# Moving a block's operand sums and its last norm to VectorE, reordering seven products, and keeping split weights in DRAM

## The chip, the cores and the metric

The kernel runs on one core of a Trainium2 chip. The metric is device time in microseconds (us) of one execution. The core has five engines that each run their own list of instructions in order: TensorE (PE, matmul; its weight loads are listed as PEld), VectorE (DVE), ScalarE (ACT), GpSimd (POOL) and SyncE (SP), which here only issues DMAs. ACT and POOL can issue DMAs too, from the same ordered list as their arithmetic.

## The reference, cut to what matters

The reference is one layer over 2048 tokens of width 1024. In short:

```python
h = layer_norm(x, emb_ln_g, emb_ln_b)
z = h @ w_in                                # 1024 x 1536: 512 columns for the S5 mixer, 1024 for the gated mixer
mix = concat(rms(s5(z[..., :512])), rms(sgu(z[..., 512:]))) @ w_out
h = layer_norm(ALPHA * h + mix, ln1_g, ln1_b)
ffn = (silu(h @ w_ffn_gate) * (h @ w_ffn_up)) @ w_ffn_down       # inner width 2816
ple = (p @ w_ple) * sigmoid(h @ w_ple_gate + b_ple_gate)
out = layer_norm(ALPHA * h + ffn + ple, ln2_g, ln2_b)
```

All of it is float32.

## The kernel before, in words

**Precision.** Each float32 product is made of three passes on TensorE (`mm3`, L69 to L71). For that every operand is split in two: a rounded high part by a cast on ScalarE (L64) and the remainder by a subtract on VectorE (L65). A tile of 128 x 512 therefore costs one cast and one subtract before PE can use it.

**Phase A (0 to about 430 us).** Four chunks of 512 tokens go through the input norm, the input projection and the gated mixer; the S5 mixer follows. `w_stream` yields 48 pieces of `w_in`, 128 x 1024 floats (512 KB) each: four for the S5 columns of chunk 0, then for each chunk eight for the gated mixer and four for the S5 columns of the next chunk; the last eight belong to chunk 3. So 12 distinct pieces come four times. Three are loaded in `norm_in`; the other 45 pass through `ahead_w`, which keeps up to three pieces ahead: a load into a `raw` buffer (3 of them, one load each), then two casts and two subtracts into two `wsp` tiles (6 of them). For five pieces (`POOL_W`) the subtract is on POOL. POOL also builds rotation tables in this phase (L683 to L703).

**Phase B (540 us to the end).** The tokens go in two blocks of 1024, block 0 and block 1, and each block is a 2 x 2 arrangement: the first and the second 512 tokens (`tg` 0 and 1), each with a left and a right half of the columns (`hf`). A large product is done with seven half-size products instead of eight (Strassen-Winograd), for which sums of operands are needed. For each block come: the gate of the `ple` branch (`ple`), eleven steps of gate and up projection with seven products each, and the down projection (`down`), where product n adds its result to one quarter of the accumulators `acc`.

**The operand sums.** `operands(blk)` loads h of the block from DRAM (`load_f`, tile `tx`, 6 buffers), splits it, and for four values of j calls `sums_B`, which forms four sums on POOL (L1358 to L1361) and splits them. For block 1 this runs while block 0 is in its down projection: `phase_b` advances it by one step after each of the seven products, but the framework that lays out the instruction lists puts work earlier where an engine has room, and in the trace all of it lies between about 1255 and 1340 us, in the first two products.

**The down projection.** `seven` runs the products in the order 0 to 6 on two sets of four PSUM banks: even ones accumulate in `u`, odd ones in `q` (1 starts one set, 3 and 5 share the next). After each product, `read` adds the four banks to `acc` on VectorE (L1500). A product is 11 steps of two operand loads on SP (L1467, L1468), two splits, and 12 matmuls. In block 1, product 6 takes its four banks one after the other, so that the token tiles of `tg` 1 finish one by one.

**The last norm.** `norm_out` has four steps `pr` of two token tiles: statistics and inverse root on VectorE; then, for all but the second half of block 1, the scaling on ScalarE (L1297) and gain and bias on POOL (L1303, L1304, 128 x 512 at a time); then the store of the tile on SP (L1306). For the second half of block 1 VectorE does it all in two instructions per 128 x 512 (`ln_apply`, L136 and L137). After product 5, `down` runs the first two steps (`tg` 0). In block 0 the other two run inside the `ple` of block 1, in block 1 after everything else. The `ple` of block 1 begins with `rows`, whose first instruction is a memset on POOL (L1263).

Of the kernel before, what the change touches and what calls it, by code (L numbers as in the profile page):

```python
# [7 lines left out]
F32 = mybir.dt.float32  # L8
F32R = mybir.dt.float32r
I32 = mybir.dt.int32  # L10
AF = mybir.ActivationFunctionType
ALU = mybir.AluOpType

P = 128
# [18 lines left out]
POOL_W = range(3, 16, 3)  # L33
# [17 lines left out]
class Kern:  # L51
# [100 lines left out]
    def run(self):  # L152
        nc, tc = self.nc, self.tc
        with ExitStack() as ctx:
# [15 lines left out]
            self.tbd = dt([NG * NS, 2, NC + 1], F32, name="tbd")  # L170
            self.hfd = dt([4, D, 512], F32, name="hfd")
            self.xnd = dt([S, D], F32, name="xnd")
            self.fod = dt([2, NP, 7, P, 512], F32, name="fod")
            self.wtd = dt([NP, 2, P, D], F32, name="wtd")
            self.pgd = dt([4, 2, P, D], F32, name="pgd")
# [170 lines left out]

    def ahead_w(self, n=W_AHEAD):
        while len(self.ahead) < n:
            w = next(self.ws, None)
            if w is not None:  # L350
                self.wi += 1
                w = self.load_split(w, 1024, self.nc.gpsimd if self.wi in POOL_W else None)
            self.ahead.append(w)

    def next_w(self):
# [776 lines left out]

    def seven(self, product, read):
        u = [self.bank() for _ in range(4)]
        product(0, u, True)
        read(0, u)
        yield
        for n in range(1, 7):  # L1140
            if n % 2:
                if n < 5:
                    q = [self.bank() for _ in range(4)]
                product(n, q, n < 5)
                read(n, q)
            else:
                product(n, u, False)
                read(n, u)
            yield

    def ple(self, blk, operands, accs):

# [51 lines left out]
                bias(ps, hf)  # L1204
                sig(tg, hf, ps, True)

        for n, _ in enumerate(self.seven(product, read)):
            yield
        for tg in range(2):
            c0 = blk * 1024 + tg * 512  # L1210
# [62 lines left out]
    def norm_out(self, blk, accs):  # L1273

        nc, v, a = self.nc, self.nc.vector, self.a
        last = blk == 1
        gb = []
        for nm in ("ln2_g", "ln2_b"):
            gb.append([self.t512() for _ in range(2)])
            for hf in range(2):  # L1280
                nc.sync.dma_start(out=gb[-1][hf],
                                  in_=a[nm][0][hf * 512:(hf + 1) * 512].unsqueeze(0).broadcast_to([P, 512]))
        for pr in range(4):
            tg, t0 = pr // 2, 2 * (pr % 2)
            xs = accs[tg][t0:t0 + 2]
            parts = [[x] for x in xs] if last and tg else [xs]
            for i, part in enumerate(parts):
                mv = self.ln_stats(part, D)
                rs = self.ln_rstd(mv)
                for j, x in enumerate(part):  # L1290
                    t = t0 + i + j
                    nb = None
                    if not (last and tg):
                        nb = self.small.tile([P, 1], F32, name="nb", tag="nb", bufs=3)
                        v.tensor_scalar(out=nb, in0=mv[:, j, 0:1], scalar1=rs[:, j:j + 1], scalar2=-1.0,
                                        op0=ALU.mult, op1=ALU.mult)
                        nc.scalar.activation(out=x, in_=x, func=AF.Identity, scale=rs[:, j:j + 1], bias=nb)  # L1297
                    for hf in range(2):
                        xh = x[:, hf * 512:(hf + 1) * 512]
                        if nb is None:  # L1300
                            self.ln_apply(xh, xh, mv[:, j, 0:1], rs[:, j:j + 1], gb[0][hf], gb[1][hf])
                        else:
                            nc.gpsimd.tensor_tensor(out=xh, in0=xh, in1=gb[0][hf], op=ALU.mult)  # L1303
                            nc.gpsimd.tensor_tensor(out=xh, in0=xh, in1=gb[1][hf], op=ALU.add)  # L1304
                    c0 = blk * 1024 + tg * 512 + t * P
                    nc.sync.dma_start(out=self.out[0][c0:c0 + P, :], in_=x)  # L1306
            yield
# [45 lines left out]
        return h  # L1353

    def sums_B(self, blk, B, j):
        g = self.nc.gpsimd
        b11, b12, b22, b21 = (self.load_f(blk, tg, k) for tg, k in ((0, j), (1, j), (1, j + 4), (0, j + 4)))
        g.tensor_tensor(out=b22, in0=b22, in1=b12, op=ALU.subtract)  # L1358
        g.tensor_tensor(out=b12, in0=b12, in1=b11, op=ALU.subtract)
        g.tensor_tensor(out=b11, in0=b22, in1=b11, op=ALU.add)  # L1360
        g.tensor_tensor(out=b21, in0=b21, in1=b11, op=ALU.subtract)  # L1361
        for i, t in ((3, b12), (4, b11), (5, b22), (6, b21)):
            B[i][j] = self.split_f(t, self.hTt() if 4 * j + i - 3 < 14 else self.hxt())
# [91 lines left out]
    def down(self, blk, accs, tail):  # L1455
# [40 lines left out]
        def read(n, ps):  # L1496
            tg, hf = ((0, 0), (0, 0), (0, 1), (1, 1), (1, 1), (0, 1), (1, 0))[n]
            for t in range(4):
                x = accs[tg][t][:, hf * 512:(hf + 1) * 512]
                v.tensor_tensor(out=x, in0=x, in1=ps[t], op=ALU.add)  # L1500

        for n, _ in enumerate(self.seven(product, read)):
            if n == 5:
                next(tail)
                next(tail)
            yield

# [29 lines left out]
```

## Time and profile before

| | us |
|---|---|
| median of three runs (lowest, highest) | 2291.97 (2288.82, 2292.2) |
| the profiled execution | 2291.72 |
| its span in the trace | 2289.9 |
| PE busy | 2160.6 |
| DVE busy | 1569.8 |
| ACT busy | 887.6 |
| POOL busy | 671.6 |
| mean granted TensorE clock | 0.978 |

The span is what the trace covers from the first to the last recorded work; the profiled execution lasted 1.8 us longer. A matmul of 512 columns is listed with some 0.39 us, but they overlap: in an undisturbed stretch of 20 us about 90 of them start, one each 0.22 us. So the number of matmuls in a stretch tells more about lost time than PE's busy time.

### The profile page before, as it was taken

What the parts mean: (1) busy time and instruction counts of PE and PEld (TensorE: products, weight loads), DVE (VectorE), ACT (ScalarE), POOL (GpSimd) and SP (SyncE); (2) the same over time, 40 slices, a digit from 0 to 9 for tenths busy, and PEclk for the clock granted to TensorE, in tenths of its full rate; (3) what the DMA queues carried; (4) which work ended last, traced back from release to release, by engine and by line L of the source; (5) the groups of instructions that cost most, each with busy time, mean ns of one, the idle gap of its engine ahead of it and who ended that gap; (6) DMA issues with size and microseconds to landing.
All of it is one profiled execution on the core that took longest, in us unless ns stands there. A gap on an engine that the chain in (4) does not pass through costs nothing.

```text
span 2289.9 us, 27942 instructions
## 1 busy us (share of the span) xinstructions
PE 2160.6 (94%) x9556; PEld 1762.1 (77%) x9556; DVE 1569.8 (69%) x2724; ACT 887.6 (39%) x1511; POOL 671.6 (29%) x602
## 2 busy tenths in 40 slices
PE   7899998899899899999999889989999999999996
PEld 6777887777677778888888668868788888878885
DVE  7997779777786455666666675663576767665559
ACT  4444554353324433232323444444333333324442
POOL 1187200000004024454545220052246455410004
PEclk9999999999999999999999999989999999999998
DMA  8546444547975434545454766543243434346563
GB/s 268 148 152 219 139 139 143 154 113 239 312 249 202 156 127 135 175 161 180 165 172 164 249 201 207 183 138 129 79 143 120 143 115 144 101 139 211 193 200 131
DMA packets 314124, 385.81 MB, mean 168 GB/s; under 512 B 62406, under 2 KB 180214, under 8 KB 313980
## 3 DMA queue, kind: packets, MB, share of 16 engines
q1 hardware_dynamic: 262812, 318.45, 43.3%
q10 hardware_dynamic: 50080, 61.36, 7.6%
q0 software_dynamic: 1088, 4.21, 0.5%
q8 instruction: 75, 1.23, 0.2%
q14 instruction: 69, 0.57, 0.1%
HBM read 273.30 MB, written 110.64 MB: 168 GB/s over the span
## 4 chain that ended last, share of the span: by engine, by line
PE 66%; DVE 14%; DMA 8%; issue 7%; POOL 3%; ACT 2%; SPq 0%; ACTq 0%; DVEq 0%; POOLq 0%
PE ps L69 21%; PE ps L70 21%; PE ps L71 21%; DMA tx<-hfd 1%; DVE st L116 1%; DVE wsp L65 1%; DMA raw<-md 1%; PE ps L143 1%; DVE z L912 1%; DMA U<-ud 1%; DVE hTx L65 1%; POOL acc L1303 1%; DVE hT L65 1%; DVE acc L1044 1%; POOL acc L1304 0%
## 5 line engine op out<-in xcount | busy, mean ns | idle before, releaser
L65 DVE TENSOR_TENSOR wsp<-raw,wsp 128x512 fp32r<-128x512 f32 x463 | 397.1, 865 | 296.3 <-ACT wsp L64 291.2
L64 ACT CAST wsp<-raw 128x512 fp32r<-128x512 f32 x473 | 290.6, 622 | 559.5 <-PE ps L71 348.3
L69 PE MATMUL ps<-hT,wsp 128*128 128x512 f32 x744 | 290.7, 391 | 6.0 <-ACT hT L312 6.0
L70 PE MATMUL ps<-hT,wsp 128*128 128x512 f32 x744 | 290.4, 391 | 1.0 <-DVE hT L313 1.0
L71 PE MATMUL ps<-hT,wsp 128*128 128x512 f32 x744 | 290.0, 390 | 0.0
L69 PE MATMUL ps<-wsp,ff 128*128 128x512 f32 x636 | 252.0, 396 | 20.7 <-ACT ff L64 20.7
L71 PE MATMUL ps<-wsp,ff 128*128 128x512 f32 x636 | 251.2, 396 | 6.7 <-DVE ff L65 6.6
L70 PE MATMUL ps<-wsp,ff 128*128 128x512 f32 x636 | 251.0, 395 | 0.2 <-DVE wsp L65 0.2
L69 PE MATMUL ps<-hTx,wsp 128*128 128x512 f32 x616 | 241.5, 392 | 5.7 <-DVE tx L1406 3.7
L70 PE MATMUL ps<-hTx,wsp 128*128 128x512 f32 x616 | 239.9, 389 | 0.0
L71 PE MATMUL ps<-hTx,wsp 128*128 128x512 f32 x616 | 239.7, 389 | 0.0
L64 ACT CAST wsp<-S 128x512 fp32r<-128x512 f32 x158 | 97.9, 620 | 240.6 <-PE ps L71 162.2
L1373 POOL TENSOR_TENSOR S<-raw 128x512 f32<-128x512 f32 x44 | 68.5, 1557 | 408.6 <-DVE wsp L65 258.6
L70 PE MATMUL ps<-wsp,hT 128*128 128x512 f32 x416 | 165.1, 397 | 6.0 <-DVE wsp L65 6.0
L69 PE MATMUL ps<-wsp,hT 128*128 128x512 f32 x416 | 165.8, 399 | 4.8 <-DVE z L912 4.8
L65 DVE TENSOR_TENSOR wsp<-S,wsp 128x512 fp32r<-128x512 f32 x158 | 129.7, 821 | 56.3 <-ACT wsp L64 54.3
L69 PEld LDWEIGHTS ps<-hT,wsp 128*128 128x128 f32 x744 | 140.2, 188 | 35.3 <-ACT hT L312 6.5
L71 PE MATMUL ps<-wsp,hT 128*128 128x512 f32 x416 | 164.5, 395 | 0.0
L70 PEld LDWEIGHTS ps<-hT,wsp 128*128 128x128 f32 x744 | 140.2, 188 | 31.0 <-DVE hT L313 2.2
L71 PEld LDWEIGHTS ps<-hT,wsp 128*128 128x128 f32 x744 | 140.1, 188 | 29.0
L69 PEld LDWEIGHTS ps<-wsp,ff 128*128 128x128 f32 x636 | 121.6, 191 | 48.9 <-ACT ff L64 24.2
L1303 POOL TENSOR_TENSOR acc<-acc,t 128x512 f32<-128x512 f32 x24 | 36.7, 1547 | 398.4 <-ACT acc L1297 398.4
(345 smaller groups left out, 4267.6 us busy)
## 6 DMA issues: line engine op xcount, KB each, us to landing
raw<-fod SPq DMA_DIRECT2D x126, 256.0 KB
raw<-in_w_in_dram SPq DMA_DIRECT2D x48, 512.0 KB
raw<-in_w_ffn_gate_dram SPq DMA_DIRECT2D x44, 512.0 KB
raw<-in_w_ffn_up_dram SPq DMA_DIRECT2D x44, 512.0 KB
fod<-tx ACTq DMA_DIRECT2D x88, 256.0 KB
raw<-wtd SPq DMA_DIRECT2D x72, 256.0 KB
fod<-ff ACTq DMA_DIRECT2D x66, 256.0 KB
tx<-hfd SPq DMA_DIRECT2D x56, 256.0 KB
```

What stands on the lines that cost most here:

```text
L64: nc.scalar.copy(out=hi, in_=src)
L65: (e or nc.vector).tensor_tensor(out=lo, in0=src, in1=hi.bitcast(F32), op=ALU.subtract)
L69: mm(ps, lhsT=lh, rhs=rh, start=start, stop=False, skip_group_check=more)
L70: mm(ps, lhsT=lh, rhs=rl, start=False, stop=False, skip_group_check=more)
L71: mm(ps, lhsT=ll, rhs=rh, start=False, stop=stop, skip_group_check=more)
L116: nc.vector.bn_stats(out=st[:, c, :], in_=t[:, c * 512:(c + 1) * 512])
L143: self.nc.tensor.transpose(ps[:, t * P:(t + 1) * P], x[:, col:col + P], self.ident)
L912: v.scalar_tensor_tensor(out=mx[:, ct, :].rearrange("p (c s) -> p s c", s=L), in0=yT[ct].rearrange("p (s c) -> p s c", s=L), scalar=self.g ...
L1044: v.tensor_tensor(out=x, in0=x, in1=ag0, op=ALU.mult)
L1303: nc.gpsimd.tensor_tensor(out=xh, in0=xh, in1=gb[0][hf], op=ALU.mult)
L1373: g.tensor_tensor(out=s1, in0=a21, in1=a22, op=ALU.add)
```

## The change

It has three parts.

1. `ahead_w`: the 12 pieces of `w_in` numbered 4 to 15 (chunk 0's gated mixer and chunk 1's S5 columns) are loaded and split as before, and the two split tiles of each are also stored to a new DRAM buffer `wsd`, by DMAs that ScalarE issues. From piece 16 on (32 pieces) nothing is split: SP loads the two finished `wsp` tiles (512 KB each) straight from `wsd`.
2. `seven` takes the order as an argument. `ple` keeps 0 to 6; `down` uses 0, 1, 2, 3, 5, 4, 6. The first two steps of the last norm come one after product 5 and one after product 4, instead of both after product 5.
3. `norm_out` always uses `ln_apply` on VectorE; `sums_B` of block 1 is on VectorE (that of block 0 stays on POOL).

```diff
             self.xnd = dt([S, D], F32, name="xnd")
+            self.wsd = dt([12, 2, P, 2, 512], F32, name="wsd")
...
         while len(self.ahead) < n:
-            w = next(self.ws, None)
-            if w is not None:
+            src = next(self.ws, None)
+            w = None
+            if src is not None:
                 self.wi += 1
-                w = self.load_split(w, 1024, self.nc.gpsimd if self.wi in POOL_W else None)
+                at = self.wsd[(self.wi - 4) % 12] if self.wi > 3 else None
+                if self.wi < 16:
+                    w = self.load_split(src, 1024, self.nc.gpsimd if self.wi in POOL_W else None)
+                    if at is not None:
+                        for i, t in enumerate(w.tiles):
+                            self.nc.scalar.dma_start(out=at[i], in_=t.bitcast(F32))
+                else:
+                    w = Wide([self.wspt() for _ in range(2)])
+                    for i, t in enumerate(w.tiles):
+                        self.nc.sync.dma_start(out=t.bitcast(F32), in_=at[i])
             self.ahead.append(w)
...
-    def seven(self, product, read):
...
+    def seven(self, product, read, order):
+        for n in order:
+            start = n in (0, 1, 3)
+            if start:
+                ps = [self.bank() for _ in range(4)]
+                if n == 0:
+                    u = ps
+                else:
+                    q = ps
+            ps = q if n % 2 else u
+            product(n, ps, start)
+            read(n, ps)
+            yield n
...
                 for j, x in enumerate(part):
                     t = t0 + i + j
-                    nb = None
-                    if not (last and tg):
-                        nb = self.small.tile([P, 1], F32, name="nb", tag="nb", bufs=3)
-                        v.tensor_scalar(out=nb, in0=mv[:, j, 0:1], scalar1=rs[:, j:j + 1], scalar2=-1.0,
-                                        op0=ALU.mult, op1=ALU.mult)
-                        nc.scalar.activation(out=x, in_=x, func=AF.Identity, scale=rs[:, j:j + 1], bias=nb)
                     for hf in range(2):
                         xh = x[:, hf * 512:(hf + 1) * 512]
-                        if nb is None:
-                            self.ln_apply(xh, xh, mv[:, j, 0:1], rs[:, j:j + 1], gb[0][hf], gb[1][hf])
-                        else:
-                            nc.gpsimd.tensor_tensor(out=xh, in0=xh, in1=gb[0][hf], op=ALU.mult)
-                            nc.gpsimd.tensor_tensor(out=xh, in0=xh, in1=gb[1][hf], op=ALU.add)
+                        self.ln_apply(xh, xh, mv[:, j, 0:1], rs[:, j:j + 1], gb[0][hf], gb[1][hf])
...
     def sums_B(self, blk, B, j):
-        g = self.nc.gpsimd
+        g = self.nc.vector if blk else self.nc.gpsimd
...
-        for n, _ in enumerate(self.seven(product, read)):
-            if n == 5:
-                next(tail)
+        for n in self.seven(product, read, (0, 1, 2, 3, 5, 4, 6)):
+            if n in (5, 4):
                 next(tail)
             yield
```

## Rows read from the trace of the kernel before

**Rows 1.** The page, part 1: busy time, share of the span, instructions.

```profile
PE 2160.6 (94%) x9556; PEld 1762.1 (77%) x9556; DVE 1569.8 (69%) x2724; ACT 887.6 (39%) x1511; POOL 671.6 (29%) x602
```

**Rows 2.** Stretches: length, PE, PEld, DVE, ACT, POOL busy (count), clock, DMA share, GB/s.

```profile
1260.00:1280.00 20.00, 16.69 (x74) 13.32 (x72) 16.23 (x27) 8.07 (x14) 0.00 (x0) 1.00 0.70 206
1280.00:1300.00 20.00, 18.53 (x69) 14.74 (x70) 12.07 (x18) 9.90 (x18) 6.03 (x4) 0.83 0.85 303
1300.00:1320.00 20.00, 17.20 (x74) 13.56 (x74) 10.72 (x15) 8.14 (x15) 5.89 (x4) 1.00 0.75 258
1320.00:1340.00 20.00, 13.43 (x47) 9.27 (x47) 19.58 (x19) 10.98 (x21) 13.11 (x8) 0.83 0.52 167
1500.00:1520.00 20.00, 10.68 (x34) 7.31 (x33) 5.25 (x6) 5.50 (x8) 13.04 (x10) 0.80 0.43 146
1520.00:1540.00 20.00, 20.00 (x78) 16.23 (x77) 18.65 (x62) 8.76 (x13) 3.04 (x3) 0.86 0.47 158
1540.00:1560.00 20.00, 20.00 (x88) 16.01 (x87) 10.37 (x13) 9.72 (x14) 19.74 (x14) 1.00 0.29 106
2050.00:2070.00 20.00, 16.22 (x64) 12.61 (x63) 13.11 (x20) 7.43 (x13) 0.00 (x0) 0.91 0.81 277
2070.00:2090.00 20.00, 20.00 (x90) 16.57 (x89) 11.34 (x18) 9.03 (x16) 0.00 (x0) 1.00 0.64 208
```

**Rows 3.** A wait, 1255 to 1345: who waited for whom, total us, times, longest.

```profile
ACT hT L64 <- POOL tx L1359: 9.6, 4, 3.3
```

**Rows 4.** Groups of instructions, whole span: busy us, mean ns, idle before.

```profile
L1358 POOL TENSOR_TENSOR tx<-tx 128x512 f32<-128x512 f32 x8 | 12.1, 1516 | 87.9 <-DMA tx<-hfd 78.9 <-DMA raw<-fod 9.0
L1449 DVE TENSOR_TENSOR tx<-tx 128x512 f32<-128x512 f32 x22 | 15.0, 684 | 0.0
```

**Rows 5.** Waits, 1480 to 1530, SP's own first.

```profile
SPq L1306 <- POOL acc L1304: 21.4, 4, 6.1
...
ACT wsp L64 <- DMA raw<-wtd: 9.1, 1, 9.1
```

**Rows 6.** Group of the last norm's gain on POOL (the bias is alike).

```profile
L1303 POOL TENSOR_TENSOR acc<-acc,t 128x512 f32<-128x512 f32 x24 | 36.7, 1547 | 398.4 <-ACT acc L1297 398.4
```

**Rows 7.** Timeline of the end: start us, us, engine, instruction.

```profile
2271.75 0.39 PE L71 MATMUL ps<-hTx 128*128 128x512 f32 x1
2277.69 0.68 DVE L1500 TENSOR_TENSOR acc<-acc,ps 128x512 f32<-128x512 f32 x1
2284.60 1.42 DVE L137 SCALAR_TENSOR_TENSOR acc<-acc,rs,t 128x512 f32<-128x512 f32 x2
```

**Rows 8.** Timeline of product 5's end; then one wait of the whole span.

```profile
2235.26 3.39 DVE L65 TENSOR_TENSOR hT<-raw,hT 128x512 fp32r<-128x512 f32 x5 [0.58 <-ACT hT L64]
2238.06 0.39 PE L69 MATMUL ps<-hT 128*128 128x512 f32 x1
2238.56 2.47 DVE L1500 TENSOR_TENSOR acc<-acc,ps 128x512 f32<-128x512 f32 x4
...
PE ps L69 <- DVE tx L1406: 3.7, 10, 0.4
```

**Rows 9.** Stretches of phase A, columns as in the first such group.

```profile
40.00:125.00 85.00, 76.41 (x359) 62.44 (x359) 83.16 (x223) 38.36 (x63) 22.40 (x41) 0.94 0.57 172
125.00:205.00 80.00, 73.70 (x346) 60.87 (x345) 64.06 (x119) 35.16 (x59) 66.35 (x123) 0.96 0.57 178
285.00:430.00 145.00, 133.86 (x673) 111.05 (x672) 126.48 (x273) 70.18 (x169) 2.23 (x6) 0.99 0.50 147
148.00:158.00 10.00, 10.00 (x59) 8.65 (x57) 5.80 (x13) 6.28 (x12) 9.22 (x35) 1.00 1.02 386
```

**Rows 10.** Phase A: a timeline row, a group (125 to 205 us), a DMA issue.

```profile
178.83 0.79 PE L70 MATMUL ps<-wsp,hT 128*128 128x512 f32 x1 [5.03 <-DVE wsp L65]
...
L65 DVE TENSOR_TENSOR wsp<-raw,wsp 128x512 fp32r<-128x512 f32 x23 | 17.1, 770 | 10.4 <-ACT wsp L64 10.4
...
1266.46 0.33 ACTq L1434 DMA_DIRECT2D fod<-tx  x1
```

More of the change, by code (lines that the diff above doesn't have):

```diff
@@ L1131, in down_sums @@
         self.nc.sync.dma_start(out=self.wtd[i, 1], in_=rB)
-    def seven(self, product, read):
[L1136 to L1145, printed above, removed]
-            else:
-                product(n, u, False)
-                read(n, u)
-            yield
+    def seven(self, product, read, order):
[11 more added lines that the diff above has]
+            yield n
     def ple(self, blk, operands, accs):
@@ L1205, in read @@
                 sig(tg, hf, ps, True)
-        for n, _ in enumerate(self.seven(product, read)):
+        for _ in self.seven(product, read, range(7)):
             yield
@@ L1291, in norm_out @@
                     t = t0 + i + j
-                    nb = None
-                    if not (last and tg):
-                        nb = self.small.tile([P, 1], F32, name="nb", tag="nb", bufs=3)
-                        v.tensor_scalar(out=nb, in0=mv[:, j, 0:1], scalar1=rs[:, j:j + 1], scalar2=-1.0,
-                                        op0=ALU.mult, op1=ALU.mult)
-                        nc.scalar.activation(out=x, in_=x, func=AF.Identity, scale=rs[:, j:j + 1], bias=nb)
                     for hf in range(2):
                         xh = x[:, hf * 512:(hf + 1) * 512]
-                        if nb is None:
-                            self.ln_apply(xh, xh, mv[:, j, 0:1], rs[:, j:j + 1], gb[0][hf], gb[1][hf])
-                        else:
-                            nc.gpsimd.tensor_tensor(out=xh, in0=xh, in1=gb[0][hf], op=ALU.mult)
-                            nc.gpsimd.tensor_tensor(out=xh, in0=xh, in1=gb[1][hf], op=ALU.add)
+                        self.ln_apply(xh, xh, mv[:, j, 0:1], rs[:, j:j + 1], gb[0][hf], gb[1][hf])
                     c0 = blk * 1024 + tg * 512 + t * P
@@ L1500, in read @@
                 v.tensor_tensor(out=x, in0=x, in1=ps[t], op=ALU.add)
-        for n, _ in enumerate(self.seven(product, read)):
-            if n == 5:
-                next(tail)
+        for n in self.seven(product, read, (0, 1, 2, 3, 5, 4, 6)):
+            if n in (5, 4):
                 next(tail)
```

## The prediction

> **What bounds the kernel now.** The first view is the page's busy times: PE is busy for 94% of the span, VectorE for 69% [rows 1]. So the time is PE's work plus the stretches in which PE is held up, and a change that takes no matmul away can only win from those. The table of 20 us stretches shows where they are. An undisturbed stretch of the down projection starts 90 matmuls, one each 0.222 us; I count every missing one as 0.222 us, which takes in both idle time and a lower granted clock (0.80 to 0.91 in the disturbed stretches) [rows 2]. The four stretches from 1260 to 1340 us (entry of block 0's down projection, with block 1's operand sums) miss 16 + 21 + 16 + 43 = 96 matmuls, 21.3 us. The two from 1500 to 1540 (its end, with the last norm of its first half) miss 56 + 12 = 68, 15.1 us. Block 1's entry, which has no operand sums beside it, misses 26, 5.8 us. A few matmul records can be missing from a trace, so these are good to about 1 us. The changed parts lie in just these places, at the very end, and in phase A.
>
> **Operand sums of block 1.** Added to VectorE: 4 x 4 = 16 instructions. That PE loses 21.3 us here and only 5.8 us at block 1's entry leaves 15.5 us to what runs beside it, and the waits name it: ScalarE's casts of the sums wait 9.6 us for POOL's second instruction alone [rows 3], and behind these casts in ScalarE's list stand the casts for the down products. A POOL instruction takes 1516 ns, the same on VectorE 684 ns [rows 4], so the four chains get 16 x 0.83 = 13.3 us shorter. VectorE had 80 - 58.6 = 21.4 us idle in the four stretches [rows 2] and is asked for 16 x 0.684 = 10.9 us more. Upper end: all 15.5 us. Lower end: -6 us, since POOL stood idle for loads of h before its first instruction (78.9 us over the run [rows 4]); on VectorE that wait would stand ahead of the splits, and one such stall can cost what the entry of block 1 costs, 5.8 us. What stays late is SP, whose loads of h wait for `tx` buffers with loads of down operands behind them; these buffers come free sooner. I take **9 us gained**.
>
> **Last norm of block 0.** SP's list waited 21.4 us in four pieces for POOL's gain and bias before it could issue the output stores, and behind these stores stood the operand loads of product 6 and the first loads of the next `ple`: ScalarE waited 9.1 us for one such load [rows 5]. POOL ran 16 instructions of some 1.55 us in a row, 24.8 us [rows 6], after ScalarE's scalings. On VectorE they are 16 of 1.42 / 2 = 0.71 us [rows 7], 11.4 us, 5.7 us per step; the scalings go. The memset on POOL with which `rows` begins is no longer queued behind the norm. The first half's last product moves from the sixth place to the fifth, one place and not two; its second step still comes after the sixth product. A product is 132 matmuls, 29.3 us, in which VectorE, busy 11.34 of 20 us [rows 2], has some 12.7 us to spare; 5.7 us fit, with statistics and roots (which were VectorE's before) spread over two products. If they do not fit and all 11.4 us come before splits that PE waits for, 15.1 - 11.4 = 3.7 us are left; the upper end is 15.1 us. I take **11 us gained**, nearer to the upper end because the wait on POOL that held SP goes altogether. The last two steps run beside block 1's `ple`, where POOL's work is hidden now; VectorE has to take 11.4 us there too, and I cost it at nothing because in the stretch after it VectorE is busy 10.37 of 20 us with PE at its full rate there [rows 2]; if that cover is not there, it is part of the lower end.
>
> **The end.** PE's last matmul ends at 2271.75 + 0.39 = 2272.1 us, the span at 2289.9: 17.8 us. VectorE begins to add the last bank only at 2277.69, 5.5 us after it could, because it is behind; its last instruction ends at 2286.0, and the store takes the other 3.9 us [rows 7]. Now one of the two steps of the first half lies a product earlier, POOL is silent, and VectorE takes 8 x 0.71 = 5.7 us of applies for the other. At most the 5.5 us go, at least nothing. I take **4 us gained**.
>
> **Product 5 behind 3, and 6 behind 4.** The old order alternates the bank sets; the new one goes on in the set that was just used, so PE must wait until `read` has added the first bank. Queued behind that wait on PE is the whole next product. Two joints per block, four in all. At the old joint PE was already in the next product at 2238.06 when the reads began at 2238.56, and a read takes 2.47 / 4 = 0.6 us; before them stood a run of splits of 3.39 us [rows 8]. Where PE already continues in a bank just read, the wait was at most 0.4 us [rows 8]. So a joint costs 0.4 us if VectorE is free, 1.1 us as in this row, and up to 4.0 us behind such a run: 1.6 to 16 us. I take 0.8 us each, **3 us lost**.
>
> **Split weights in DRAM (phase A).** (a) Chunk 0, 40 to 125 us: 24 stores of 512 KB, 12.6 MB, are added to a stretch in which the DMA engines are busy 0.57 x 85 = 48.5 us [rows 9]. At the 386 GB/s of a full stretch [rows 9] they take 32.6 us more, 81 of 85 us: it just fits. ScalarE issues them, at 0.33 us [rows 10] 8 us in all, and each waits for a subtract of VectorE, which is busy 83.16 of the 85 us [rows 9]; behind it stand the casts of the next weights and activations. ScalarE has half its time free, so I take 3 us lost, from 0 to 8. (b) From chunk 1 on, 64 casts and 64 subtracts go, 23 subtracts (17.1 us) of them between 125 and 205 us [rows 10]. PE lost there 6.3 us idle and 80 x 0.04 = 3.2 us of clock [rows 9]; the one large gap, 5.03 us, is a wait for just such a subtract [rows 10], which stood behind the mixer's norm. 5 us gained, from 0 to 9.5. (c) The S5 stretch from 285 us: VectorE is busy 126 of 145 us and PE idle for 11 us [rows 9]; up to 16 subtracts of 0.68 us leave it or lie just before it. 3 us gained, from 0 to 11. (d) A piece is now 1 MB and is loaded only once its `wsp` tiles are free, two pieces or 48 x 0.222 = 10.7 us ahead, with no `raw` buffers in front, and an SP wait for a tile holds the x, U and CS loads behind it. At 386 GB/s it takes 2.7 us. 2 us lost, from 0 to 5, the size of the gap in (b). Together **3 us gained**.
>
> **Sum.** 9 + 11 + 4 - 3 + 3 = 24 us. Against the profiled execution, 2291.7 (span 2289.9 and 1.8 around it): **2267.7, say 2268 us**. The median before is 0.3 us higher, so nothing has to be rescaled.
>
> **Rivals.**
> First, slower: **the stores fill the DMA queues in chunk 0**. Loads and stores share the same engines. If the 12.6 MB move not at 386 GB/s but at the stretch's present mean of 172 GB/s, they take 73 us, and 48.5 + 73 = 121.5 us of work lies in 85 us: 36.5 us late instead of the 3 us in the sum, so 2268 + 33.5 = 2301 us. It decides from where the loss reaches 27 us, 63.5 us of stores, below 198 GB/s. For it speaks that this stretch moves many small packets; against it, that the full-rate row is from the same phase, and that weights are loaded well ahead. On this the Trainium skill ("DMA: Bandwidth & Descriptors", section "Queues, rings and completion order") speaks against the change: queues of different issuers are rows on the same 16 engines, served in turn packet by packet, so stores issued by ScalarE would halve the rate of SP's weight loads as long as both are queued. No row here shows two full queues side by side. I give this rival 0.14.
> Second, no change: **VectorE becomes the bound** of the down projections. The sums then give -2, the norm 3.7, the end 0, with -3 for the joints and 3 for phase A: 1.7 us gained, 2290 us. For it: statistics, roots and applies of a step fill nearly all of the 12.7 us spare time. Against it: only two of a block's seven products carry such a step, and the sums' 10.9 us meet 21.4 us in which VectorE was idle. 0.14.
> Third, **one of the two main terms fails**: SP stays clogged at the entry by loads of h (sums 0, 2277 us), or the norm's stores still hold up the loads (norm 4, 2275 us). About 2276 us, 0.17.
> Fourth, the change does not do what it says: the list order is not the program order, and the framework may put the first half's norm where it was. That costs the end's 4 us, 2272 us, inside the forecast's own range.
>
> **How the numbers follow.** Forecast, 2268 us with 2254 to 2281 as its own range: 0.53. With the third rival 0.70. The remaining 0.02 is for less than 2252. The range reaches up to the second rival: 2252 to 2291, which leaves out the first rival and some of the tail below. A measurement of this kernel can tell about 0.2% (4.6 us) from no change. Faster by more: 0.53 + 0.17 + 0.02 and 0.02 of the second rival, 0.74. Within: 0.10 of the second. Slower: the first, and 0.02 of the second, 0.16.
>
> **What would show it.** The four stretches at the entry of block 0's down projection miss about 55 matmuls instead of 96; SP's wait before the output stores is gone and the stretch at the end of that projection misses under 20; from PE's last matmul to the end it is about 14 us; waits of PE for `read` appear at four joints, below 1.5 us each; chunk 0 gets a few us longer and the 5 us gap in chunk 1 is gone. Wrong would be: PE waiting for DMA of weights in phase A, subtracts of VectorE releasing PE throughout the down products, or stretches that were undisturbed before losing matmuls.

## The result, and the profile after

The changed kernel takes **2251.8 us** (median of four runs, 2248.24 to 2252.42) against 2291.7 us for the kernel before on the same chip: ratio 0.983, interval 0.981 to 0.984, 39.9 us gained. Forecast were 24 us gained, 2268 us, with 2252 to 2291 as the range: the direction holds, the gain is two thirds larger, and the median lies 0.2 us below the low end. The forecast's own range, 2254 to 2281 us, is missed too, and the prediction gave a time below 2252 us a chance of 0.02. The profiled execution took 2252.42 us, its span 2250.3.

Page of after, part 1 (busy time, share, instructions), then its 20 us stretches (length, PE, PEld, DVE, ACT, POOL busy and count, clock, DMA share, GB/s). They answer to [rows 1] and [rows 2]; block 0's last two products, which carry the two steps of the norm, now lie between about 1429 and 1490.

```profile
PE 2150.2 (96%) x9556; PEld 1759.2 (78%) x9556; DVE 1528.5 (68%) x2712; ACT 841.8 (37%) x1435; POOL 558.2 (25%) x538
```

```profile
1260.00:1280.00 20.00, 15.05 (x57) 11.38 (x56) 14.19 (x23) 6.28 (x11) 0.00 (x0) 0.91 0.76 243
1280.00:1300.00 20.00, 19.41 (x85) 15.69 (x84) 16.36 (x27) 11.39 (x20) 0.00 (x0) 1.00 0.96 325
1300.00:1320.00 20.00, 18.63 (x82) 15.10 (x81) 17.93 (x31) 12.46 (x24) 0.00 (x0) 1.00 0.73 238
1320.00:1340.00 20.00, 20.00 (x90) 16.55 (x89) 15.40 (x25) 10.23 (x18) 0.00 (x0) 1.00 0.73 238
...
1440.00:1460.00 20.00, 20.00 (x90) 16.57 (x89) 19.69 (x49) 8.94 (x16) 0.00 (x0) 1.00 0.80 269
1460.00:1480.00 20.00, 20.00 (x90) 16.58 (x89) 14.73 (x24) 8.38 (x14) 0.00 (x0) 1.00 0.57 206
1480.00:1500.00 20.00, 20.00 (x90) 16.57 (x89) 15.02 (x34) 8.67 (x13) 0.96 (x1) 1.00 0.44 134
```

The entry misses 33 + 5 + 8 + 0 = 46 matmuls instead of 96, and the end of block 0's down projection none, although VectorE is busy 19.69 of 20 us in one stretch there. ScalarE's wait for POOL's sums [rows 3] is gone; for the sums on VectorE its casts `hT` wait 5.3 us between 1255 and 1345. SP's waits before the output stores, from 1420 to 1520 (engine, line, what it waited for; total us, times, longest), are shorter than in [rows 5], not gone:

```profile
SPq L1305 <- DVE acc L137: 12.8, 7, 3.7
```

The end and the last joint (product 4 to 6 in block 1), from the timeline of after (start us, us, engine, instruction), against [rows 7] and [rows 8]:

```profile
2203.34 1.31 DVE L1499 TENSOR_TENSOR acc<-acc,ps 128x512 f32<-128x512 f32 x2
...
2204.70 1.32 DVE L1499 TENSOR_TENSOR acc<-acc,ps 128x512 f32<-128x512 f32 x2
...
2204.90 0.39 PE L71 MATMUL ps<-wsp,ff 128*128 128x512 f32 x1
2205.12 0.39 PE L69 MATMUL ps<-hT 128*128 128x512 f32 x1
...
2234.99 0.39 PE L71 MATMUL ps<-hTx 128*128 128x512 f32 x1
...
2235.42 0.69 DVE L1499 TENSOR_TENSOR acc<-acc,ps 128x512 f32<-128x512 f32 x1
...
2244.94 1.42 DVE L137 SCALAR_TENSOR_TENSOR acc<-acc,rs,t 128x512 f32<-128x512 f32 x2
```

At the joint the last matmul of product 4 starts at 2204.90 and the first of product 6 at 2205.12, the normal 0.22 us apart: the first two banks had been read (2203.34) while PE was still filling the others. At the end the last read begins as PE ends (2235.4), not 5.5 us later, and 14.9 us remain to 2250.3, against 17.8.

Phase A of after, stretches as in [rows 9]; then the new gap of PE in it, and a wait of PE in the kernel before from 40 to 125 us:

```profile
40.00:125.00 85.00, 76.00 (x344) 62.16 (x344) 79.44 (x217) 34.83 (x59) 20.27 (x35) 0.92 0.90 305
125.00:205.00 80.00, 78.57 (x383) 65.82 (x382) 51.56 (x117) 25.65 (x38) 59.90 (x142) 1.00 0.87 300
...
285.00:430.00 145.00, 135.08 (x676) 110.98 (x674) 120.12 (x265) 64.97 (x161) 2.23 (x6) 0.98 0.53 160
```

```profile
73.49 1.97 PE L143 MATMUL ps<-ident,xt 128*128 128x128 f32 x8 [5.90 <-ACT z L445]
```

```profile
PE ps L69 <- ACT hT L312: 6.0, 1, 6.0
```

Chunk 0 lost 15 matmuls (359 to 344), chunk 1 won 37 (346 to 383), the S5 stretch 3. The 5 us gap in chunk 1 [rows 10] is gone. In chunk 0 the new gap takes the place of one of 6.0 us that only before has, so the 15 are a balance: from 60 to 80 us after starts 65 matmuls against 104, from 90 to 110 us 71 against 51. The first of these stretches was undisturbed before, which the prediction had named as a sign of being wrong.

To compare kernels I cut the span at three instructions of VectorE: the first and the last up-projection sum `ff<-tx,ff` (the last is in block 1) and the first read of block 0's `down`. Lengths in us, from their start times; the rows under after are the experiments told of below:

| | start to first up sum | to first read of block 0 | to last up sum of block 1 | to the end |
|---|---|---|---|---|
| before | 892.2 | 435.9 | 726.7 | 235.1 |
| after | 886.5 | 426.2 | 709.6 | 228.0 |
| p_sums | 892.4 | 426.1 | 722.3 | 234.7 |
| p_norm | 893.5 | 435.9 | 719.5 | 237.2 |
| p_order | 890.1 | 435.7 | 721.5 | 242.9 |
| norm_order | 895.0 | 437.1 | 710.7 | 229.4 |
| p_wsd | 886.5 | 435.2 | 725.1 | 235.4 |
| u_order | 887.2 | 424.2 | 714.1 | 241.0 |
| order_both5 | 891.1 | 424.4 | 713.4 | 237.4 |
| sums_both | 874.8 | 426.5 | 707.4 | 228.4 |

After minus before: 5.7 (phase A and its surroundings), 9.7 (entry), 17.1 (block 0's down and block 1's projections), 7.1 (block 1's down and the end), 39.6 us. Each row is one execution, up to 5 us from its kernel's median (norm_order 2274.0 against 2269.12 us, sums_both 2238.89 against 2243.59). The first column varies by up to 4.9 us between kernels that are alike in phase A: 890.1 to 895.0 in the five rows without split weights in DRAM, 886.5 to 891.1 in the four with them and with block 0's sums on POOL. The means of the two groups, 892.6 and 887.8, differ by 4.8 us.

### The profile page after: what moved, and what is told of

Same layout as the page of the kernel before. It is cut to its first block, busy times and chain, and to the rows that moved or that the text cites. A ratio compares the mean times of both kernels' runs of the same rounds, so it can differ in the third digit from the quotient of the medians.

```text
span 2250.3 us, 27832 instructions
## 1 busy us (share of the span) xinstructions
PE 2150.2 (96%) x9556; PEld 1759.2 (78%) x9556; DVE 1528.5 (68%) x2712; ACT 841.8 (37%) x1435; POOL 558.2 (25%) x538
## 4 chain that ended last, share of the span: by engine, by line
PE 73%; DVE 9%; DMA 8%; issue 7%; ACT 1%; POOL 1%; SPq 0%; ACTq 0%; DVEq 0%; POOLq 0%
PE ps L69 23%; PE ps L70 23%; PE ps L71 23%; DMA raw<-md 1%; DMA tx<-hfd 1%; PE ps L143 1%; DVE st L116 1%; DMA hfd<-t 1%; DMA xt<-in_x_dram 1%; DVE z L923 1%; DMA raw<-in_w_ffn_down_dram 1%; DVE wsp L65 1%; DVE acc L1055 1%; DMA raw<-in_w_in_dram 0%; DVE hT L65 0%
## 5 line engine op out<-in xcount | busy, mean ns | idle before, releaser
L65 DVE TENSOR_TENSOR wsp<-raw,wsp 128x512 fp32r<-128x512 f32 x399 | 339.8, 857 | 238.7 <-ACT wsp L64 234.1
L64 ACT CAST wsp<-raw 128x512 fp32r<-128x512 f32 x409 | 251.9, 622 | 505.4 <-PE ps L71 304.3
L69 PEld LDWEIGHTS ps<-wsp,ff 128*128 128x128 f32 x636 | 121.1, 190 | 41.5 <-ACT ff L64 16.6
L71 PEld LDWEIGHTS ps<-wsp,ff 128*128 128x128 f32 x636 | 120.5, 189 | 28.5 <-DVE ff L65 3.5
```

Of the source, the lines that this page charges most:

```text
L64: nc.scalar.copy(out=hi, in_=src)
L65: (e or nc.vector).tensor_tensor(out=lo, in0=src, in1=hi.bitcast(F32), op=ALU.subtract)
L69: mm(ps, lhsT=lh, rhs=rh, start=start, stop=False, skip_group_check=more)
L71: mm(ps, lhsT=ll, rhs=rh, start=False, stop=stop, skip_group_check=more)
```

## The experiments

All times are medians; the kernel before ran beside each group at 2292.2 to 2292.6 us.

### The four parts alone

**p_sums**, the kernel before with one line:

```diff
-        g = self.nc.gpsimd
+        g = self.nc.vector if blk else self.nc.gpsimd
```

> The kernel before with block 1's operand sums on VectorE and nothing else. Theory (the chain POOL sum, ScalarE cast, down split holds PE): the entry of block 0's down projection misses about 46 matmuls instead of 96, 11 us gained, 2281 us. Rival (the entry got better because the other parts shifted the work there): at most 3 us gained, 2289 us or more, and still about 90 missing.

Measured 2277.17 us, ratio 0.993 (0.992 to 0.995): 15.1 us gained, 9.8 of them at the entry, 4.4 in the following stretch; the four stretches from 1260 to 1340 us miss 43 matmuls, where the theory had 46. VectorE's busy time fell from 1569.8 to 1565.6 although it has 16 instructions of 0.684 us more, 10.9 us. So other instructions got 15 us shorter. The group of splits of the summed operands, 1255 to 1345 us (busy us, mean ns, idle before), in before and in p_sums:

```profile
L65 DVE TENSOR_TENSOR hT<-tx,hT 128x512 fp32r<-128x512 f32 x14 | 14.9, 1085 | 6.9 <-ACT hT L64 6.4
```

```profile
L65 DVE TENSOR_TENSOR hT<-tx,hT 128x512 fp32r<-128x512 f32 x14 | 9.3, 687 | 0.0
```

The timeline of before shows why (a POOL sum with VectorE idle, then two POOL sums and the split of VectorE beside them):

```profile
1307.08 1.28 POOL L1359 TENSOR_TENSOR tx<-tx 128x512 f32<-128x512 f32 x1
...
1322.04 1.62 POOL L1359 TENSOR_TENSOR tx<-tx 128x512 f32<-128x512 f32 x1
...
1322.43 1.77 DVE L65 TENSOR_TENSOR wsp<-S,wsp 128x512 fp32r<-128x512 f32 x1
...
1323.74 1.62 POOL L1360 TENSOR_TENSOR tx<-tx 128x512 f32<-128x512 f32 x1
```

A split beside a POOL sum takes 1.77 us instead of 0.69, and the POOL sum 1.62 instead of 1.28; both then repeat every 1.7 us. The Trainium skill ("SBUF — State Buffer", section "SBUF: two separate sides") says that VectorE and GpSimd share a pair of ports as an exclusive lock, held for a whole instruction, which a VectorE operation with two SBUF inputs needs against a GpSimd operation that reads SBUF. These rows agree: a subtract has two such inputs, and the two engines slow each other. They don't agree to the full: a pair takes 1.70 us (1322.04 to 1323.74), less than 1.28 + 0.69 = 1.97 us, so some 0.27 us of a pair run side by side (an estimate from these rows).

**p_norm**, the kernel before with `norm_out` of after:

```diff
-                        nc.scalar.activation(out=x, in_=x, func=AF.Identity, scale=rs[:, j:j + 1], bias=nb)
...
-                            nc.gpsimd.tensor_tensor(out=xh, in0=xh, in1=gb[0][hf], op=ALU.mult)
-                            nc.gpsimd.tensor_tensor(out=xh, in0=xh, in1=gb[1][hf], op=ALU.add)
+                        self.ln_apply(xh, xh, mv[:, j, 0:1], rs[:, j:j + 1], gb[0][hf], gb[1][hf])
```

> The kernel before with the last norm of both blocks on VectorE, in the old order of the products. Theory (what costs is that SP's stores and loads wait for POOL): the 15 us at the end of block 0's down projection go, and some 1 to 3 us at the very end: 2275 us. Rival (VectorE can take it only because the new order spreads it over two products): both steps, 11.4 us, fall into one product, the splits come late, and no more than 5 us are gained: 2287 us.

Measured 2285.91 us, 0.997 (0.996 to 0.998): 6.4 us gained. A stretch of 20 us, a wait of PE and the two splits between which VectorE does not split:

```profile
1480.00:1500.00 20.00, 14.88 (x58) 11.82 (x57) 20.00 (x63) 4.31 (x8) 0.00 (x0) 0.83 0.36 122
```

```profile
PE ps L71 <- DVE ff L65: 5.1, 1, 5.1
```

```profile
1477.10 0.69 DVE L65 TENSOR_TENSOR ff<-raw,ff 128x512 fp32r<-128x512 f32 x1 [1.43 <-ACT ff L64]
1477.71 2.47 DVE L1490 TENSOR_TENSOR acc<-acc,ps 128x512 f32<-128x512 f32 x4
...
1493.47 0.69 DVE L65 TENSOR_TENSOR ff<-S,ff 128x512 fp32r<-128x512 f32 x1
```

From the end of the reads to 1493.47 VectorE does 13.4 us of norm, most of both steps, and no split; PE runs out of split operands and stands for 5.1 us. With the lower clock after it, the stretch misses 32 matmuls, 7.1 us. This is block 0. In block 1 the same run of norm makes PE wait only 1.3 us, but from PE's last matmul to the end it is 22.1 us instead of 17.8.

**p_order**, the kernel before with the new order alone (the norm stays on ScalarE and POOL):

```diff
-        for n, _ in enumerate(self.seven(product, read)):
-            if n == 5:
-                next(tail)
+        for n in self.seven(product, read, (0, 1, 2, 3, 5, 4, 6)):
+            if n in (5, 4):
                 next(tail)
```

> The kernel before with the order 0, 1, 2, 3, 5, 4, 6 and one step of the norm after each of 5 and 4, the norm on ScalarE and POOL as before. By the forecast the four joints cost 3 us, and half of the norm comes a product earlier, so that SP is held half as long at the end (7 us gained): 2288 us. Rival (the reads are done in time, a joint costs nothing): 2285 us or less, and no wait of PE for the reads in the trace. If each joint cost its upper end of 4 us: 2301 us.

Measured 2294.63 us, 1.001 (1.000 to 1.002): no gain. PE's wait at a joint (there are two of them, 15.5 us in all), SP's waits from 1460 to 1495, and the chain at the first of these joints, in order of time:

```profile
PE ps L69 <- DVE acc L1498: 15.5, 2, 7.8
```

```profile
SPq L1304 <- POOL acc L1302: 22.1, 4, 5.8
```

```profile
1478.03 0.34 SPq L1304 DMA_DIRECT2D out_dram<-acc  x1
...
1478.46 0.38 SPq L1465 DMA_DIRECT2D raw<-fod  x1
...
1481.78 0.62 ACT L64 CAST ff<-raw 128x512 fp32r<-128x512 f32 x1 [5.45 <-DMA raw<-fod]
...
1482.43 0.69 DVE L65 TENSOR_TENSOR ff<-raw,ff 128x512 fp32r<-128x512 f32 x1 [2.21 <-ACT ff L64]
...
1483.04 2.48 DVE L1498 TENSOR_TENSOR acc<-acc,ps 128x512 f32<-128x512 f32 x4
...
1483.87 0.76 PE L69 MATMUL ps<-wsp,ff 128*128 128x512 f32 x1 [7.74 <-DVE acc L1498]
```

SP's store waits for POOL's bias; the load behind it goes out at 1478.46; its split stands in VectorE's list ahead of the reads; and PE, which has to go on in the bank that is read, starts 7.74 us late. With the norm on POOL, the joint and the stores on SP make one chain. It is the same at the second of these joints, in block 1 (7.80 us); the joints of product 5 behind 3 make no such wait. From PE's last matmul to the end it is 12.1 us instead of 17.8, since half of the norm comes earlier, but PE ends 13.4 us later, counted from the last up sum.

**p_wsd**, the kernel before with `ahead_w` of after:

```diff
+                at = self.wsd[(self.wi - 4) % 12] if self.wi > 3 else None
+                if self.wi < 16:
...
+                            self.nc.scalar.dma_start(out=at[i], in_=t.bitcast(F32))
+                else:
+                    w = Wide([self.wspt() for _ in range(2)])
+                    for i, t in enumerate(w.tiles):
+                        self.nc.sync.dma_start(out=t.bitcast(F32), in_=at[i])
```

> The kernel before with the split weights kept in DRAM and nothing else. Forecast: 3 us gained, 2289 us. By the trace of the changed kernel, whose first gate product comes 5.7 us earlier: 2286 us. Rival (phase A's gain there needs the other parts, or is lost again before the first gate product): 2291 us.

Measured 2286.07 us, 0.998 (0.997 to 0.999): 6.2 us gained, 5.7 in the first column, as in after.

Alone, the parts give 15.1 + 6.4 - 2.4 + 6.2 = 25.3 us, close to the forecast's 24; together 39.9. Some 14.6 us come from two parts meeting.

### Which two parts

**u_order**, the changed kernel with the old order:

```diff
-        for n in self.seven(product, read, (0, 1, 2, 3, 5, 4, 6)):
-            if n in (5, 4):
+        for n, _ in enumerate(self.seven(product, read)):
+            if n == 5:
+                next(tail)
                 next(tail)
```

> The changed kernel with the products back in the order 0 to 6 and both steps of the norm after product 5. If the parts add up as measured alone (sums -15, norm -6, weights -6): 2265 us. Theory now (the order is worth much only with the norm on VectorE, because the output stores then wait in SP's list in short pieces): 2265 us or more, a gap of PE of some 8 us at the end of block 0's down projection, and SP waiting some 12 us in one piece before an output store. Forecast's view (the order costs 3 us): 2249 us.

Measured 2270.73 us, 0.991 (0.989 to 0.993). SP's longest wait before a store is 12.7 us, as expected, PE's gap at the end of block 0 is 5.1 us and not 8. The order, which alone gains nothing (2.4 us slower, not distinguishable from none), is worth 19.0 us with the norm on VectorE: 13.0 of it in the last column, where PE waits only 1.9 us for a split. Of these 13.0, 8.2 lie behind PE's last matmul: 23.1 us to the end against 14.9 in after.

**norm_order**, the kernel before with the norm on VectorE and the new order (the two diffs above together):

> The kernel before with two parts together: the last norm on VectorE and the new order with one step after product 5 and one after product 4; operand sums and split weights as before. Theory that the two parts help each other (the norm's instructions fit on VectorE only when the steps are spread over two products, and the spread helps only when a step is short): the norm alone gave 6.4 us and the order alone cost 2.4, the whole change has some 14.6 us more than its four parts added up, and all of that should be here: 2292 - 6.4 + 2.4 - 14.6 = 2273 to 2274 us. Theory that the surplus comes from somewhere else (sums with the split weights or with the order): the two just add, 2288 us. In between, the surplus is shared.

Measured 2269.12 us, 0.991 (0.989 to 0.992): 23.1 us gained where the two alone add to 4.0. That is 19.1 us from their meeting, all of the surplus and 4.5 us more. By columns 3.6 us of the meeting lie in the third and 15.6 in the last: p_order loses 13.4 us at block 1's joint and behind it, before PE's last matmul, p_norm has 22.1 us behind that matmul, and norm_order has neither (14.9 us). So p_sums, norm_order and p_wsd add to 44.4 us, and the whole has 39.9; in the third column they add to 22.0 us against 17.1. The intervals of these four medians, 2 to 3.5 us to either side, don't tell the 4.5 us from nothing; if the sums or the weights do bring less beside the norm, the reason stays open.

**norm_store_pool**, p_norm with block 0's output stores on POOL, so that SP holds none of them:

```diff
-                    nc.sync.dma_start(out=self.out[0][c0:c0 + P, :], in_=x)
+                    (nc.sync if last else nc.gpsimd).dma_start(out=self.out[0][c0:c0 + P, :], in_=x)
```

> The kernel before with the norm on VectorE in the old order, and block 0's output stores issued by POOL, whose list is empty there, instead of SP. Theory (SP's list, held by the stores, delays the operand loads behind them): the 8 us gap that the norm alone leaves goes, 2278 us or less. Rival (VectorE itself is full: two steps of the norm in one product delay the splits, the stores only look like it): as the norm alone, 2285 us.

Measured 2284.28 us, 0.997 (0.995 to 0.999), within the interval of p_norm. The gap is still there, the same 5.1 us:

```profile
1491.76 2.07 PE L71 MATMUL ps<-wsp,ff 128*128 128x512 f32 x4 [5.12 <-DVE ff L65]
```

SP now waits 14.7 us in one piece before an operand load, for VectorE. So the stores on SP are not what p_norm has left; VectorE's list is.

**order_both5**, the changed kernel with both steps after product 5:

```diff
-            if n in (5, 4):
+            if n == 5:
+                next(tail)
                 next(tail)
```

> The kernel after, but both steps of the first half's norm run after product 5, none after product 4 (the order 0, 1, 2, 3, 5, 4, 6 stays). Theory of a full VectorE: both steps, some 13 to 15 us of VectorE's list, stand ahead of the splits of the one product that follows, so PE gets the gap of about 5 us with a stretch at the lower clock again, 7 to 8 us in each block, while the end stays near 15 us: 2252 + 7 to 15, so 2259 to 2267 us. Theory that only the place counts (the first half done a product earlier, well before the end, with the output stores earlier too): 2250 to 2253 us.

Measured 2268.33 us, 0.990 (0.989 to 0.992): 16.6 us slower than after, just past the upper end of what the full VectorE gives (2259 to 2267 us). The order of products is that of after, only the second step lies one product earlier, and the gap is back in both blocks (stretches, then the waits of PE from 1230 us on):

```profile
1440.00:1460.00 20.00, 14.89 (x55) 11.82 (x54) 19.31 (x53) 4.15 (x7) 0.00 (x0) 0.83 0.61 214
2180.00:2200.00 20.00, 14.89 (x63) 11.99 (x62) 18.73 (x55) 4.68 (x8) 0.00 (x0) 0.92 0.35 119
```

```profile
PE ps L71 <- DVE ff L65: 10.2, 2, 5.1
```

By columns the loss is 3.8 us in the third, 9.4 in the last and 4.6 in the first, where nothing was changed; without the first it is 11.4 us. That the first half is done earlier does not prevent the gap, but it is worth something at the end: from PE's last matmul it is 11.7 us here, 23.1 in u_order and 14.9 in after. What this kernel loses in the last column it loses before that matmul, 12.6 us. So both count, the place of the first half and one step to a product.

### The stores of the split weights

**store_only**, the kernel before with the 24 stores from ScalarE and nothing read back (extra work, no use of it):

```diff
+                    if at is not None and self.wi < 16:
+                        for i, t in enumerate(w.tiles):
+                            self.nc.scalar.dma_start(out=at[i], in_=t.bitcast(F32))
```

> The kernel before with the 24 stores of split weights added, and nothing read back: all pieces are split as before. It shows what chunk 0 pays for the stores: forecast 3 us (2295 us), the first rival 36 us (2328 us); chunk 1's 5 us gap stays.

Measured 2294.08 us, 1.001 (1.000 to 1.002): 1.5 us, not distinguishable from none.

```profile
40.00:125.00 85.00, 73.75 (x341) 60.84 (x340) 80.19 (x217) 33.96 (x57) 20.89 (x33) 0.94 0.87 297
```

The stores run beside the loads at 297 GB/s over the whole stretch; 18 fewer matmuls start in it than in before (some 3.7 us), of which the whole time keeps 1.5. The other kernels without stores here start 348 to 359, those with them 328 to 344.

**wsd_pool**, the changed kernel with POOL issuing these stores:

```diff
-                            self.nc.scalar.dma_start(out=at[i], in_=t.bitcast(F32))
+                            self.nc.gpsimd.dma_start(out=at[i], in_=t.bitcast(F32))
```

> The changed kernel with the stores of split weights issued by POOL instead of ScalarE: the same bytes, another list. Theory (what costs in chunk 0 is that ScalarE's list waits for subtracts at each store, and its gelu behind it frees PE's banks late): the 5.9 us gap goes, 2247 us. Rival (the DMA traffic delays the loads): the gap stays, 2252 us; if POOL's descriptors or its waits hold up its own subtracts, slower, up to 2258 us.

Measured 2252.97 us, 0.983 (0.981 to 0.985), as after. PE's gap in chunk 0 stays:

```profile
PE ps L143 <- ACT z L445: 6.3, 1, 6.3
```

So it is not ScalarE's issuing alone that makes it. The cast ahead of the gelu waits 10.3 us for a weight load here, as the rival (delayed loads) has it, and such waits are 20.5 us in this stretch. But store_only and p_wsd have a gap of 5.3 us in the same place with only 1.0 and 0.6 us of them. What makes the gap where ScalarE issues stays open.

**wsd_late**, the changed kernel with stores in chunk 1 (pieces 16 to 27) and loads from piece 28 on:

```diff
-                at = self.wsd[(self.wi - 4) % 12] if self.wi > 3 else None
-                if self.wi < 16:
+                at = self.wsd[(self.wi - 4) % 12] if self.wi > 15 else None
+                if self.wi < 28:
```

> The kernel after, but the split weights are stored in the stretch of chunk 1 (pieces 16 to 27) and read back from piece 28 on; chunk 0 is as in the kernel before. Theory that the 12.6 MB of stores in chunk 0 are what costs PE 15 matmuls and the 6 us gap there: chunk 0 returns to 359 matmuls in its 85 us, 3 us won back, and chunk 1, whose DMA engines are no busier, has splits and stores instead of loads: its gap of 4 to 5 us returns, and 12 pieces fewer come without a split. Sum about 2253 to 2256 us. Theory that the stores cost nothing anywhere: chunk 0 unchanged and the gap in chunk 1 back, 2257 us or more.

Measured 2262.86 us, 0.987 (0.986 to 0.989): slower than the 2253 to 2256 us of the first theory; the second theory (2257 us or more) has the time right, but not that chunk 0 stays as in after. Chunk 0 and chunk 1:

```profile
40.00:125.00 85.00, 76.33 (x359) 62.44 (x358) 83.92 (x226) 38.25 (x63) 21.81 (x40) 0.96 0.62 189
125.00:205.00 80.00, 72.04 (x326) 58.51 (x326) 57.16 (x106) 32.08 (x55) 65.96 (x125) 0.94 0.80 288
```

Chunk 0 is back at 359 matmuls, so the stores do cost 15 there. But chunk 1 starts 57 fewer than in after and 20 fewer than in before: the stores cost about as much in either chunk, and the splits that the early storing takes out of chunk 1 are worth more than I had put down.

### A faster version

**sums_both**, the changed kernel with block 0's sums on VectorE as well:

```diff
-        g = self.nc.vector if blk else self.nc.gpsimd
+        g = self.nc.vector
```

> The kernel after with the operand sums of block 0 on VectorE as well (16 instructions more there). In after, the stretches from 700 to 760 us, where these sums are on POOL, start 90, 80 and 57 matmuls, so some 43 are missing against 90 each, 9.5 us. Theory that the chain through POOL (16 instructions of some 1.5 us against 0.69) is what is late there: 3 to 9 us gained, 2243 to 2249 us. Theory that PE's wait in that place is for the ple accumulators, which VectorE itself finishes (a wait of 7.1 us in the trace of after), so that 11 us more on VectorE only stand in front of it: no gain or a loss, 2252 to 2260 us.

Measured **2243.59 us**, 0.979 (0.977 to 0.981), 8.2 us better than after. The stretches where these sums run, in after and in sums_both:

```profile
720.00:740.00 20.00, 18.52 (x80) 14.46 (x78) 15.78 (x18) 7.68 (x15) 11.80 (x8) 1.00 0.32 102
740.00:760.00 20.00, 12.76 (x57) 10.15 (x58) 16.31 (x39) 8.98 (x16) 0.00 (x0) 0.83 0.60 217
```

```profile
720.00:740.00 20.00, 20.00 (x87) 16.17 (x87) 19.91 (x38) 10.57 (x19) 0.00 (x0) 1.00 0.29 93
740.00:760.00 20.00, 19.59 (x101) 15.37 (x100) 9.04 (x22) 10.39 (x16) 0.00 (x0) 1.00 0.80 283
```

PE starts 51 matmuls more in the two stretches. Of these 39 have 512 columns, 8.7 us; the others are short transposes, the last of which starts 9.5 us earlier (753.9 instead of 763.4). The first column is 11.7 us shorter, in an execution that was 4.7 us faster than the median. VectorE took on 16 instructions and its busy time is the same 1528.5 us: the splits `hT<-tx` take 685 ns in the mean instead of 838. The gain is near the top of what the first theory gave; the second, more work in front of a wait that VectorE itself ends, falls.

## Why the prediction was right in direction and short in size

**Sums: 9 us forecast, 15.1 measured alone.** The chain was right (POOL's sums hold ScalarE's casts, which hold the down products), and the term's upper end, 15.5 us, came out. I took 9 because VectorE would be asked for 10.9 us more. That step failed: VectorE was not asked for more at all, since the splits beside POOL had taken up to 1.77 us instead of 0.69. The entry still misses 46 matmuls where I expected 55.

**Last norm of block 0: 11 us forecast; 7.2 alone in the third column, 16.0 with the order.** That SP's stores waited for POOL with operand loads behind them was right: p_order shows the whole chain. "5.7 us fit", spread over two products, was right too, and it hung on that spread. Two steps are 13.4 us of VectorE in a row and do not fit in block 0 (p_norm, u_order, order_both5: each a 5.1 us gap); one does. In after the steps leave no more than 3.6 and 5.3 us between two splits, reads included. The 16.0 us lie just past the term's upper end, 15.1. The spread comes with the order; the forecast had counted on it here and at the end, and had set the joints against it as a cost.

**Product 5 behind 3, and 6 behind 4: -3 us forecast, 0 in after.** PE has no wait for a read there. With the norm on POOL two joints cost 7.7 and 7.8 us, beyond the upper end of 4.0, because the reads stood behind a split that waited for a load. The price of a joint depends on what is ahead of the read in VectorE's list, and the norm's move took the wait of 22.1 us for POOL, which made that split late, out of SP's list. The forecast priced a joint by itself, as a loss whatever becomes of the norm; the two together are worth 19.1 us more than the sum of each alone.

**The end: 4 us forecast, 7.1 in the last column.** From PE's last matmul to the end it is 14.9 us (about 14 forecast), 2.9 us of the gain. The rest lies before PE's last matmul: in before, the stretches from 2230 to 2270 us start 82 and 81 matmuls, 17 missing, 3.8 us, and in after there is no such loss (90 and 89 from 2190 to 2230 us). The forecast read only what came after PE. The two stretches of before:

```profile
2230.00:2250.00 20.00, 18.49 (x82) 14.94 (x81) 17.95 (x55) 11.88 (x20) 0.00 (x0) 1.00 0.60 201
2250.00:2270.00 20.00, 18.51 (x81) 14.63 (x80) 19.78 (x48) 3.90 (x4) 19.53 (x13) 1.00 0.14 55
```

**Phase A: 3 us forecast, 5.7 measured** (4.8 by the means of the first column, 6.2 by p_wsd alone). (a) Chunk 0 lost 15 matmuls at 0.2 us (the undisturbed chunk 2 starts 390 in 80 us), 3 us, as forecast; the DMA share is 0.90 where I worked out 81 of 85 us. (b) Chunk 1 won 37, some 7.5 us against 5. (c) The S5 stretch won 3 matmuls, 0.7 us against 3. (d) PE waits once for a weight load, 1.4 us.

**Rivals.** The first, stores that fill the DMA queues, falls: store_only costs 1.5 us, not 36.5 us. In chunk 0 ScalarE waits for weight loads 6.5 us in before and 9.5 in after, 20.5 in wsd_pool, but 1.0 in store_only and 0.6 in p_wsd, so the waits don't show whether the stores slow the loads. The Trainium skill's rule of queues served in turn ("DMA: Bandwidth & Descriptors", section "Queues, rings and completion order") would have these loads at half rate while both queues are full; no run here shows how long a single load took, and the 1.5 us show how little of it can have reached PE. The second, VectorE as the bound, is what happens in p_norm and u_order for some 20 us at block 0's end and in order_both5 at both blocks' ends; the spread over two products takes it away. The third and the fourth did not occur: SP's waits at the stores shrank, and the trace shows one step after product 5 and one after product 4.

**Gap between the forecast and the time.** By columns: entry and the stretch behind it 9.7 + 4.4 = 14.1 us (4.4 by p_sums) against 9, block 0's end 17.1 - 4.4 = 12.7 against 9.5 (half of the joints put here), the end 7.1 against 2.5, phase A 5.7 against 3: 39.6 against 24. Every term came out on the same side; the sums and the end are the furthest off, 5.1 and 4.6 us.

## What to carry over

Price work that two engines do side by side by what it costs both: the busy time of VectorE in a stretch with POOL at work contains waiting, and moving POOL's element-wise work to VectorE can leave VectorE less busy. When a change moves work onto an engine whose in-order list also feeds the bound engine, count how long the new run of instructions is without a feeding one between them, and compare it with how far ahead that engine works; spreading it can be worth as much as moving it. Two parts that touch the same list are to be priced together, since each can take away the obstacle of the other.

## What the runs showed of the hardware that was not expected

A VectorE subtract of 128 x 512 takes 0.69 us alone and 1.77 us beside a POOL operation of the same size; POOL's takes 1.28 us with VectorE idle and 1.62 beside it. A PE gap of 5.1 us costs more than itself: the stretch of order_both5 with it is granted 0.83 of the full clock (part of it at the lower of the two levels) and starts 55 matmuls instead of 90, 7.8 us, and right behind the gap matmuls last 0.63 us instead of 0.39:

```profile
1447.79 2.08 PE L71 MATMUL ps<-wsp,ff 128*128 128x512 f32 x4 [5.11 <-DVE ff L65]
...
1449.66 0.63 PE L69 MATMUL ps<-wsp,ff 128*128 128x512 f32 x1
```
